# A one-core streaming-encoder step: gating's small products in larger groups, the rows' norm one piece later, k and v copied raw out of PSUM

## The chip, the core and the metric

The kernel runs on one NeuronCore of a Trainium2 chip. The metric is the device time of one execution in microseconds (us). TensorE (PE) multiplies out of SBUF into PSUM; VectorE (DVE), ScalarE (ACT) and GpSimd (POOL) do the elementwise work; SyncE (SP) issues nearly all loads and stores. PEld is TensorE's loading of a stationary operand, which the profile lists apart from the matmul itself. A PSUM tile of 128 x 512 f32 is called a bank here.

## The reference

One layer of a streaming encoder over 256 prompt frames and 64 sample frames (T = 320 columns in all, stored as columns; the 2048 features lie on partitions in 16 tiles of 128):

```python
z = rmsnorm(x, ln_mix_g) @ w_in                  # 2048 -> 3328: q 1024, k 128, v 128, u 1024, v_gate 1024
q, k = rmsnorm(q, q_g), rmsnorm(k, k_g)          # per head of 64
a = windowed_attention(q, k, v, rel_bias, sinks) # 16 heads, 2 kv heads, chunks of 64, band of 192 keys
u, vg = gelu(z_u), rmsnorm(gelu(z_v), g)
s = u * (W_s @ vg + b_s)                         # 8 channel groups, over 128 positions, masked
x = x + concat(rmsnorm(a, g_a), rmsnorm(s, g_s)) @ w_out
x = x + square(relu(rmsnorm(x, ln_ffn) @ w_up)) @ w_down   # 2048 -> 8192 -> 2048
```

Outputs are the new x, the new k and v rows, and the normalised gate rows of the sample frames.

## The kernel before

Every large product keeps 256 output features in PSUM as two banks of 128 x 320 (`acc`, two such tiles in rotation) and reads its weights in **pieces** of 512 features x 256 columns: one DMA (`w_raw`), a rounded copy on ACT (`w_hi`, L108) and the remainder on DVE (`w_lo`, L109), three buffers of each. The activations are split in the same way (XH and XL, FH and FL). A piece is then 24 matmuls of 128x128 by 128x320: 4 feature tiles x 2 halves x 3 terms (hi.hi, hi.lo, lo.hi), all at L134. A product over 2048 features is four pieces.

The program runs in this order. (1) The first pass (L220 to L241) computes q's first 256 columns into `q0_ps` and k and v into `kv_ps`, an `acc` tile, while x itself arrives. (2) `q1`, `q2`, `q3`, each a product of four pieces. (3) Four gate products `v0` to `v3`, then four `u0` to `u3`, each followed by a gelu (`gelu2`). (4) w_out in two halves. (5) The feed-forward, 128 products, with the last one in two separate banks (`apart`).

The small work is fitted **between pieces**: `between_pieces` names, per piece, a function whose matmuls go in behind that piece's 24. `attend(i)` there issues three stages of three different attention blocks: `values_of` (block i-3, L448), `scores` (block i, L392) and `turn` (block i-2, L435, transposes). The last two of them are `attend(11)` and `attend(12)`. Gating's own small work is: `rstd_rows(acc_v)` (L159, the row norm of the gate values, six tiny matmuls and a DVE and a POOL instruction, which give `rv`), `by_rows` (L512, 24 transposes in groups of four, each group into one bank and out by an ACT copy that scales with `rv`), and `spatial` (L526 and L528, three matmuls for each of eight channel groups into one bank, which two DVE additions, L529 and L532, empty). In `u_pieces` the row norm stands directly behind `attend(11)`, at the end of u0.

PSUM is shared out as: two `acc` tiles (four banks), one two-bank tile in the pool `ps_sc` (tag `s_ps`: `q0_ps`, then the scores, and the output `o_ps` of the last attention blocks), and two single banks from `misc()`, for which all other small products take turns.

The mean square of x comes only after the first pass: `rstd` (L167) gives `rx` by a chain of eleven DVE instructions while q1 runs. k and v are multiplied by `rx` out of `kv_ps` (L335, L336), and only then is that `acc` tile free for q2.

Each engine works through its own list in order, and the lists are set when the kernel is built, by a scheduler that estimates times and obeys the hints `issue_after` (behind that instruction in the order; it puts no wait into the program by itself) and `keep_in_program_order`. SP's list is one chain: weight loads with up to four small loads (`between`) behind each.

Of the kernel before, what the change touches and what calls it, by code (L numbers as in the profile page):

```python
# [8 lines left out]
F32 = mybir.dt.float32  # L9
F32R = mybir.dt.float32r  # L10
I32 = mybir.dt.int32
AF = mybir.ActivationFunctionType
ALU = mybir.AluOpType
AX = mybir.AxisListType

P = 128
T = 320
TP = 384
TT = [(0, 128), (128, 128), (256, 64)]
# [4 lines left out]
EPS = 1e-6  # L24
# [6 lines left out]
def hymba_step_kernel(ctx: ExitStack, tc: tile.TileContext, i, o):  # L31
    nc = tc.nc
# [4 lines left out]
    sm = ctx.enter_context(tc.tile_pool(name="sm", bufs=2))  # L37
# [7 lines left out]
    def misc():  # L45
        return ps_m.tile([P, 512], F32, name="misc", tag="misc")
# [9 lines left out]
    xT = const.tile([P, KT, T], F32, name="xT")  # L56
# [5 lines left out]
    tab = const.tile([32, 16], F32, name="tab")  # L62
    oneh = sm.tile([32, 255], F32, name="oneh", tag="w1", bufs=3)
    nc.scalar.dma_start(out=cols, in_=i["cols"])
    nc.gpsimd.dma_start(out=oneh, in_=i["onehot"])
    nc.gpsimd.dma_start(out=tab, in_=i["table"])

    ident = const.tile([P, P], F32, name="ident")
    make_identity(nc, ident)
    nhalf = const.tile([P, 16], F32, name="nhalf")  # L70
    nc.vector.memset(nhalf, -0.5)
    warm = const.tile([P, 1], F32, name="warm")
    nc.scalar.activation(out=warm, in_=nhalf[:, 0:1], func=AF.Exp)
    idle = sm.tile([P, T], F32, name="idle", tag="w1", bufs=3)
    nc.vector.memset(idle, 0.0)
    warm_ps = misc()
    for _ in range(3):
        nc.tensor.matmul(out=warm_ps[:, 0:256], lhsT=idle[:, 0:128], rhs=idle[:, 0:256], start=True, stop=True)
# [119 lines left out]
    def rstd_b(name):  # L198
        return sm.tile([P, T], F32, name=name, tag="rstd_b", bufs=2)
# [16 lines left out]
    kv_ps = acc_tile()  # L216
# [3 lines left out]
    for a, n in [(a, 1) for a in range(8)] + [(a, 2) for a in range(8, KT, 2)]:  # L220
        if a % 4 == 0:
            ahead = blk("w_first", [P, 2, 4, 256])
        raw = ahead[:, :, a % 4:a % 4 + n]
        load(xT[:, a:a + n], xv[:, a:a + n])
        for k in range(n if a else 0):
            load(raw[:, :, k], wv[:, a + k, 0:2048].rearrange("p (j c) -> p j c", j=2)[:, :, 0:256])
        for k in range(a, a + n):
            split(xT[:, k], g_mix[:, k:k + 1], XH[:, k], XL[:, k], pinned=True)
        hi, lo = [t.rearrange("p (j k) c -> p j k c", j=2)[:, :, 0:n] for t in w_tiles()]
        if a:  # L230
            high, low = halves(raw, hi, lo, pinned=True)
        else:
            for j in range(2):
                load(raw[:, j, 0], wv[:, 0, j * 1024:j * 1024 + 256])
                high, low = halves(raw[:, j, 0], hi[:, j, 0], lo[:, j, 0], pinned=True)

        for x, (w_, r_) in enumerate(((hi, xh), (hi, xl), (lo, xh))):
            for j, k, g in [(j, k, g) for j in range(2) for k in range(n) for g in range(2)]:
                ps = q0_ps if j == 0 else kv_ps
                mm = nc.tensor.matmul(out=ps[:, g, 0:T], lhsT=w_[:, j, k, g * P:(g + 1) * P], rhs=r_(a + k),  # L240
                                      start=(a + k == 0 and x == 0), stop=(a + k == KT - 1 and x == 2))  # L241
        steps.append((high, low, mm.ins))
        if a == 5:
            b_ps = misc()
            with tc.issue_after(mm.ins):
                nc.tensor.matmul(out=b_ps[0:16, 0:255], lhsT=tab, rhs=oneh, start=True, stop=True)
        if a == 7:
            b_row = sm.tile([16, 255], F32, name="b_row", tag="w1", bufs=3)
            with tc.issue_after(low):
                nc.vector.tensor_copy(out=b_row, in_=b_ps[0:16, 0:255])  # L250
            b_dram = dram.tile([16, 15, 255], F32, name="b_dram")
            nc.gpsimd.dma_start(out=b_dram, in_=b_row[:, None, :].to_broadcast([16, 15, 255]))
# [9 lines left out]
    vz = kzv[:, 896:1664].rearrange("p (x h d) -> p x h d", x=6, h=2)  # L262
    cv = i["cv"].rearrange("k (h d) -> k h d", h=2)
    vC = vz[:, 5]
    nc.gpsimd.dma_start(out=vC[0:96], in_=cv[0:96])
    sinks = at.tile([P, 8], F32, name="sinks", bufs=1)
    nc.sync.dma_start(out=sinks, in_=i["sinks"])

# [25 lines left out]
    ssq = sums("ssq")  # L294
    nc.vector.tensor_tensor(out=ssq, in0=ssq2[:, 0], in1=ssq2[:, 1], op=ALU.add)

    rk, rx = rstd_b("rk"), rstd_b("rx")

    rq = at.tile([P, 4, 10], F32, name="rq", bufs=1)
# [31 lines left out]
    q1_ps = product(w_in, 0, KT, 256, xh, xl, between_pieces={0: lambda: rstd(ssq, mean_dm, EPS, rx)},  # L331
                    halves_behind={2: lambda: rests[-1]})

    zk = sm.tile([P, T], F32, name="zk", tag="w2", bufs=4)
    nc.vector.tensor_tensor(out=zk, in0=kv_ps[:, 0, 0:T], in1=rx, op=ALU.mult)  # L335
    nc.vector.tensor_tensor(out=vT, in0=kv_ps[:, 1, 0:T], in1=rx, op=ALU.mult)  # L336
    ksq = sums("ksq")
    nc.scalar.activation(out=ksq, in_=zk, func=AF.Square)  # L338
    q0_sq = evict_q(0, q0_ps)
# [114 lines left out]
    def attend(i):  # L454

        for stage, u in ((values_of, i - 3), (scores, i), (turn, i - 2)):
            if 0 <= u < 10:
                with tc.issue_after(narrow[-1]):
                    stage(u)
# [44 lines left out]
    nc.gpsimd.memset(vnat_s[HD:P], 0.0)  # L504
    rv = []

    def by_rows(*ths):

        for t, h in ths:
            (t0, n), vps = TT[t], misc()  # L510
            for a in range(4):
                mm = nc.tensor.transpose(out=vps[0:n, a * P:(a + 1) * P], in_=gv[:, 4 * h + a, t0:t0 + n],  # L512
                                         identity=ident)
            dst = vnat[:, t] if t < 2 else vnat_s[0:HD]
            nc.scalar.activation(out=dst[:, h * 512:(h + 1) * 512], in_=vps[0:n], func=AF.Copy,
                                 scale=rv[0][0:n, t:t + 1])
        narrow.append(mm.ins)
        if ths[-1] == (2, 1):
            nc.gpsimd.dma_start(out=o["sgu_v"], in_=vnat_s[0:HD])

    def spatial(*gs):
        for g in gs:
            sp_ps = misc()
            cs = slice(g * P, (g + 1) * P)
            for b in range(2):
                nc.tensor.matmul(out=sp_ps[:, b * P:(b + 1) * P], lhsT=vnat[:, b, cs], rhs=wsT[:, g], start=True,  # L526
                                 stop=True)
            mm = nc.tensor.matmul(out=sp_ps[:, 256:T], lhsT=vnat_s[:, cs], rhs=wsT[:, g, 0:HD], start=True, stop=True)  # L528
            nc.vector.tensor_tensor(out=gv[:, g, 0:256].rearrange("p (b i) -> p b i", b=2),  # L529
                                    in0=sp_ps[:, 0:256].rearrange("p (b i) -> p b i", b=2),  # L530
                                    in1=sgb[:, g, None, :].to_broadcast([P, 2, P]), op=ALU.add)
            nc.vector.tensor_tensor(out=gv[:, g, 256:T], in0=sp_ps[:, 256:T], in1=sgb[:, g, 0:HD], op=ALU.add)  # L532
        narrow.append(mm.ins)

    def last_values():
        attend(11)
        with tc.issue_after(narrow[-1]):
            rv.append(rstd_rows(acc_v, inv_1k, 4 * EPS))

    acc_s = sums("acc_s")  # L540
    rs_a, rm_a = [], rstd_b("rm_a")
    u_pieces = {
        0: {1: lambda: attend(10), 3: last_values},
        1: {0: lambda: by_rows((0, 0), (1, 0)), 1: lambda: (attend(12), by_rows((2, 0), (0, 1))),
            2: lambda: by_rows((1, 1), (2, 1)), 3: lambda: spatial(0, 1)},
        2: {0: lambda: spatial(2, 3), 1: lambda: spatial(4, 5), 2: lambda: spatial(6, 7)},
        3: {0: lambda: rs_a.append(rstd_rows(acc_a, inv_1k, EPS)), 2: lambda: spread(rs_a[0], rm_a)}}
    gus = {}

# [58 lines left out]
    for b in range(nb):  # L608
        FH = [blk(f"FH{h}", [P, 8, T], F32R) for h in range(2)]
        FL = [blk(f"FL{h}", [P, 8, T], F32R) for h in range(2)]  # L610
        for g in range(FB // 2):
            ps = product(i["w_up"], 0, KT, (b * FB + 2 * g) * P, hh_, hl_, wf)
            t = sm.tile([P, 2, T], F32, name="tf", tag="w2", bufs=4)
            nc.vector.scalar_tensor_tensor(out=t, in0=ps[:, :, 0:T], scalar=0.0, in1=r2[:, None, :].to_broadcast([P, 2, T]),  # L614
                                           op0=ALU.max, op1=ALU.mult)
            nc.scalar.activation(out=t, in_=t, func=AF.Square)
            fs = slice(2 * (g % 4), 2 * (g % 4) + 2)
            fh, fl = FH[g // 4][:, fs], FL[g // 4][:, fs]
            nc.scalar.activation(out=fh, in_=t, func=AF.Copy)
            nc.vector.tensor_tensor(out=fl, in0=t, in1=fh.bitcast(F32), op=ALU.subtract)  # L620
        fh_, fl_ = (lambda k: FH[k // 8][:, k % 8]), (lambda k: FL[k // 8][:, k % 8])
        for g in range(8):
            last, end = b == nb - 1, b == nb - 1 and g == 7
            ps = product(i["w_down"], b * FB, FB, g * 256, fh_, fl_, wf, apart=end)
            parts = [(2 * g, 1, ps[0][:, None, 0:T]), (2 * g + 1, 1, ps[1][:, None, 0:T])] if end else \
                [(2 * g, 2, ps[:, :, 0:T])]
            for a, n, p in parts:
                nc.vector.tensor_tensor(out=xT[:, a:a + n], in0=xT[:, a:a + n], in1=p, op=ALU.add)  # L628
                if last:
                    nc.sync.dma_start(out=yv[:, a:a + n], in_=xT[:, a:a + n])  # L630


def _onehot():
# [63 lines left out]
```

## Time and profile before

| | |
|---|---|
| median of 3 runs | 1252.55 us (1251.66 to 1254.9) |
| the profiled execution | 1251.18 us, of which its span is 1249.4 |
| PE busy | 1243.7 us |
| DVE, ACT, POOL busy | 650.8, 489.4, 102.1 us |
| TensorE clock granted | 1.0 |
| HBM read, written | 182.91 MB, 3.32 MB |

A busy PE in this table isn't PE at its peak: a matmul's row overlaps that of the next. Of use are the starts of its rows, and the chain of waits, in which each row stands from the end of the one before. In a row of the timeline the first number is the start, the second the length, both in us; brackets hold the idle time before it and what ended it.

### The profile page before, as it was taken

How to read it: one execution, taken by the hardware profiler on the slowest of the kernel's cores; microseconds unless marked ns; L12 is line 12 of the kernel's file. 1: busy time of each engine (PE TensorE's matmuls, PEld its weight loads, DVE VectorE, ACT ScalarE, POOL GpSimd, SP SyncE). 2: the span in 40 equal slices, each digit the busy share in tenths (PEclk: the TensorE clock that was granted, in tenths of full speed). 3: DMA queues.
4: the chain of work that ended last, by engine and by line, in shares of the span. 5: the costliest groups of instructions: out<-in, count | busy, mean ns of one | idle time of the engine just before them, and what ended most of it. 6: DMA issues, size and time to landing. Idle time of an engine off the chain costs nothing.

```text
span 1249.4 us, 20216 instructions
## 1 busy us (share of the span) xinstructions
PE 1243.7 (100%) x8519; PEld 1231.9 (99%) x8519; DVE 650.8 (52%) x767; ACT 489.4 (39%) x638; POOL 102.1 (8%) x97
## 2 busy tenths in 40 slices
PE   9999999999999999999999999999999999999998
PEld 8999989999999999999999999999999999999998
DVE  7868675776874444444444444444444444444443
ACT  7345555424544332333344223333332233443221
POOL 1224552301300000000000000000000000000000
PEclk9999999999999999999999999999999999999999
DMA  8644333644554444445544444555444445544550
GB/s 276 208 144 119 102 105 108 220 151 152 152 151 148 151 147 148 152 152 152 151 150 146 148 148 152 152 151 151 150 146 148 149 152 152 152 151 158 169 165 33
DMA packets 186555, 187.78 MB, mean 150 GB/s; under 512 B 6592, under 2 KB 185984, under 8 KB 186464
## 3 DMA queue, kind: packets, MB, share of 16 engines
q1 hardware_dynamic: 185824, 185.43, 47.8%
q8 instruction: 66, 1.08, 0.4%
q0 software_dynamic: 496, 1.03, 0.3%
q14 instruction: 25, 0.20, 0.0%
q10 hardware_dynamic: 144, 0.03, 0.0%
HBM read 182.91 MB, written 3.32 MB: 149 GB/s over the span
## 4 chain that ended last, share of the span: by engine, by line
PE 97%; DMA 2%; SPq 1%; ACT 0%; DVE 0%; issue 0%; ACTq 0%; DVEq 0%
PE acc L134 91%; PE misc L134 1%; DMA w_raw<-in_w_in 1%; SPq L103 1%; PE misc L435 1%; PE s_ps L392 1%; DMA b_dram<-b_row 1%; PE q_ps L240 0%; PE acc L240 0%; PE misc L448 0%; PE misc L314 0%; PE misc L526 0%; PE misc L512 0%; DMA cols<-in_cols 0%; ACT w_hi L108 0%
## 5 line engine op out<-in xcount | busy, mean ns | idle before, releaser
L109 DVE TENSOR_TENSOR w_lo<-w_raw,w_hi 128x1024 fp32r<-128x1024 f32 x332 | 413.7, 1246 | 434.6 <-ACT w_hi L108 425.1
L108 ACT ACTIVATE w_hi<-w_raw 128x1024 fp32r<-128x1024 f32 x332 | 351.8, 1060 | 699.8 <-PE acc L134 660.2
L134 PE MATMUL acc<-H2H,w_hi 128*128 128x320 f32 x1024 | 316.4, 309 | 0.0
L134 PE MATMUL acc<-H2L,w_hi 128*128 128x320 f32 x1024 | 316.4, 309 | 0.0
L134 PE MATMUL acc<-H2H,w_lo 128*128 128x320 f32 x1024 | 316.4, 309 | 0.0
L134 PE MATMUL acc<-FH,w_hi 128*128 128x320 f32 x992 | 306.5, 309 | 0.0
L134 PE MATMUL acc<-FL,w_hi 128*128 128x320 f32 x992 | 306.5, 309 | 0.0
L134 PE MATMUL acc<-FH,w_lo 128*128 128x320 f32 x992 | 306.5, 309 | 0.0
L134 PEld LDWEIGHTS acc<-H2L,w_hi 128*128 128x128 f32 x1024 | 192.3, 188 | 0.0
L134 PEld LDWEIGHTS acc<-H2H,w_hi 128*128 128x128 f32 x1024 | 192.3, 188 | 0.0
L134 PEld LDWEIGHTS acc<-H2H,w_lo 128*128 128x128 f32 x1024 | 192.3, 188 | 0.0
L134 PEld LDWEIGHTS acc<-FH,w_hi 128*128 128x128 f32 x992 | 186.2, 188 | 0.0
L134 PEld LDWEIGHTS acc<-FL,w_hi 128*128 128x128 f32 x992 | 186.2, 188 | 0.0
L134 PEld LDWEIGHTS acc<-FH,w_lo 128*128 128x128 f32 x992 | 186.2, 188 | 0.0
L134 PE MATMUL acc<-XH,w_hi 128*128 128x320 f32 x352 | 111.1, 316 | 0.1
L134 PE MATMUL acc<-XL,w_hi 128*128 128x320 f32 x352 | 108.7, 309 | 0.0
L134 PE MATMUL acc<-XH,w_lo 128*128 128x320 f32 x352 | 108.6, 309 | 0.0
L134 PEld LDWEIGHTS acc<-XH,w_hi 128*128 128x128 f32 x352 | 66.2, 188 | 0.6 <-ACT ksq L338 0.4
L134 PEld LDWEIGHTS acc<-XL,w_hi 128*128 128x128 f32 x352 | 66.2, 188 | 0.0
L134 PEld LDWEIGHTS acc<-XH,w_lo 128*128 128x128 f32 x352 | 66.0, 188 | 0.0
L614 DVE SCALAR_TENSOR_TENSOR tf<-acc,r 128x640 f32<-128x640 f32 x32 | 26.4, 825 | 41.9 <-PE acc L134 41.8
L628 DVE TENSOR_TENSOR xT<-xT,acc 128x640 f32<-128x640 f32 x31 | 25.5, 821 | 41.8 <-PE acc L134 41.8
(206 smaller groups left out, 1054.8 us busy)
## 6 DMA issues: line engine op xcount, KB each, us to landing
w_raw<-in_w_up SPq DMA_DIRECT2D x128, 512.0 KB
w_raw<-in_w_down SPq DMA_DIRECT2D x128, 512.0 KB
w_raw<-in_w_in SPq DMA_DIRECT2D x44, 512.0 KB
w_raw<-in_w_out SPq DMA_DIRECT2D x32, 512.0 KB
w_first<-in_w_in SPq DMA_DIRECT2D x15, 256.0 KB
out_yT<-xT SPq DMA_DIRECT2D x7, 320.0 KB
xT<-in_xT SPq DMA_DIRECT2D x8, 160.0 KB
xT<-in_xT SPq DMA_DIRECT2D x4, 320.0 KB
```

The costliest lines, as they stand in the source:

```text
L103: loads.append(nc.sync.dma_start(out=o_, in_=i_))
L108: return (pin(nc.scalar.activation(out=hi, in_=raw, func=AF.Copy)).ins, pin(nc.vector.tensor_tensor(out=lo, in0=raw, in1=hi.bitcast(F32), ...
L109: pin(nc.vector.tensor_tensor(out=lo, in0=raw, in1=hi.bitcast(F32), op=ALU.subtract)).ins)
L134: mm = nc.tensor.matmul(out=out, lhsT=w_[:, k, g * P:(g + 1) * P], rhs=r_(kk), start=(kk == 0 and x == 0), stop=(kk == nk - 1 and x == 2))
L392: mm = nc.tensor.matmul(out=s_ps[:, p, j * nk:(j + 1) * nk], lhsT=qT[hs, blk_, a:a + 2].rearrange("p a t -> p (a t)"), rhs=kz[hs, kv, k0:k ...
L435: mm = nc.tensor.transpose(out=pt_ps[0:n, (2 * p + j) * P:(2 * p + j + 1) * P], in_=s[:, p, j, c:c + n], identity=ident)
L614: nc.vector.scalar_tensor_tensor(out=t, in0=ps[:, :, 0:T], scalar=0.0, in1=r2[:, None, :].to_broadcast([P, 2, T]), op0=ALU.max, op1=ALU.mult)
L628: nc.vector.tensor_tensor(out=xT[:, a:a + n], in0=xT[:, a:a + n], in1=p, op=ALU.add)
```

## The change

Five things are changed.

1. `rstd_rows(acc_v)` leaves the end of u0 (behind `attend(11)`) and goes one piece later, behind u1's first piece. The transposes of `by_rows`, before in three groups of eight, become a group of sixteen with `attend(12)` behind u1's second piece and one of eight behind its third.
2. `spatial` runs four channel groups at a time, behind u1's last piece and u2's first, in place of two at a time over four pieces. For more than two groups the third and fourth bank are those of the `s_ps` tile (`banks`).
3. k and v are copied out of `kv_ps` by ACT without the norm, into a new tile `kv` (L300 to L302 of the changed kernel); the two multiplications by `rx` then read that tile, and k's is in place.
4. The hints on three small loads on POOL's queue (`onehot`, `table`, the cached values) are later ones; the zeros for the first idle matmuls are written first, and are 256 columns wide.
5. The last output tile is added and stored in two halves of 160 columns, so that there are two DVE additions and two stores where there was one of each.

```diff
-    nc.gpsimd.dma_start(out=oneh, in_=i["onehot"])
-    nc.gpsimd.dma_start(out=tab, in_=i["table"])
-
+
+    idle = sm.tile([P, 256], F32, name="idle", tag="w1", bufs=3)
+    nc.vector.memset(idle, 0.0)
...
+        if a == 1:
+            with tc.issue_after(low):
+                nc.gpsimd.dma_start(out=oneh, in_=i["onehot"])
+                nc.gpsimd.dma_start(out=tab, in_=i["table"])
...
-    nc.gpsimd.dma_start(out=vC[0:96], in_=cv[0:96])
+    with tc.issue_after(steps[-1][1]):
+        nc.gpsimd.dma_start(out=vC[0:96], in_=cv[0:96])
...
+    kv = sm.tile([P, 2, T], F32, name="kv", tag="w2", bufs=4)
+    with tc.issue_after(steps[-1][0]):
+        nc.scalar.activation(out=kv, in_=kv_ps[:, :, 0:T], func=AF.Copy)
...
-    zk = sm.tile([P, T], F32, name="zk", tag="w2", bufs=4)
-    nc.vector.tensor_tensor(out=zk, in0=kv_ps[:, 0, 0:T], in1=rx, op=ALU.mult)
-    nc.vector.tensor_tensor(out=vT, in0=kv_ps[:, 1, 0:T], in1=rx, op=ALU.mult)
+    zk = kv[:, 0]
+    nc.vector.tensor_tensor(out=zk, in0=zk, in1=rx, op=ALU.mult)
+    nc.vector.tensor_tensor(out=vT, in0=kv[:, 1], in1=rx, op=ALU.mult)
...
+    def banks(n):
+
+        if n > 2:
+            ps = ps_sc.tile([P, 2, 512], F32, name="s_ps", tag="s_ps")
+        return [misc() if x < 2 else ps[:, x - 2] for x in range(n)]
+
     def by_rows(*ths):
 
-        for t, h in ths:
-            (t0, n), vps = TT[t], misc()
+        for (t, h), vps in zip(ths, banks(len(ths))):
+            t0, n = TT[t]
...
     def spatial(*gs):
-        for g in gs:
-            sp_ps = misc()
+        for g, sp_ps in zip(gs, banks(len(gs))):
...
-    def last_values():
-        attend(11)
-        with tc.issue_after(narrow[-1]):
-            rv.append(rstd_rows(acc_v, inv_1k, 4 * EPS))
+    def rows_norm():
+        rv.append(rstd_rows(acc_v, inv_1k, 4 * EPS))
...
-        0: {1: lambda: attend(10), 3: last_values},
-        1: {0: lambda: by_rows((0, 0), (1, 0)), 1: lambda: (attend(12), by_rows((2, 0), (0, 1))),
-            2: lambda: by_rows((1, 1), (2, 1)), 3: lambda: spatial(0, 1)},
-        2: {0: lambda: spatial(2, 3), 1: lambda: spatial(4, 5), 2: lambda: spatial(6, 7)},
+        0: {1: lambda: attend(10), 3: lambda: attend(11)},
+        1: {0: rows_norm, 1: lambda: (attend(12), by_rows((0, 0), (1, 0), (2, 0), (0, 1))),
+            2: lambda: by_rows((1, 1), (2, 1)), 3: lambda: spatial(0, 1, 2, 3)},
+        2: {0: lambda: spatial(4, 5, 6, 7)},
...
-            parts = [(2 * g, 1, ps[0][:, None, 0:T]), (2 * g + 1, 1, ps[1][:, None, 0:T])] if end else \
-                [(2 * g, 2, ps[:, :, 0:T])]
-            for a, n, p in parts:
-                nc.vector.tensor_tensor(out=xT[:, a:a + n], in0=xT[:, a:a + n], in1=p, op=ALU.add)
+            parts = [(slice(2 * g, 2 * g + 2), slice(0, T), ps[:, :, 0:T])] if not end else \
+                [(2 * g, slice(0, T), ps[0][:, 0:T])] + \
+                [(2 * g + 1, c, ps[1][:, c]) for c in (slice(0, T // 2), slice(T // 2, T))]
+            for a, c, p in parts:
+                nc.vector.tensor_tensor(out=xT[:, a, c], in0=xT[:, a, c], in1=p, op=ALU.add)
                 if last:
-                    nc.sync.dma_start(out=yv[:, a:a + n], in_=xT[:, a:a + n])
+                    nc.sync.dma_start(out=yv[:, a, c], in_=xT[:, a, c])
```

**ACT at the end of the first pass, before:** two weight copies for q1 stand ahead of the row norm's `n_hl`, and the square of k (`ksq`, L338) stands behind three more.

```order
L108 ACTIVATE w_hi<-w_raw 128x1024 x2
L172 ACTIVATE n_hl<-ssq 128x320
L108 ACTIVATE w_hi<-w_raw 128x1024 x3
L338 ACTIVATE ksq<-zk 128x320
L108 ACTIVATE w_hi<-w_raw 128x1024
L308 ACTIVATE qsq<-qT 128x640
L172 ACTIVATE n_hl<-ksq 128x320
```

The same place in the changed kernel (`kv<-acc` is the new copy of k and v):

```order
L106 ACTIVATE w_hi<-w_raw 128x1024
L302 ACTIVATE kv<-acc 128x640
L170 ACTIVATE n_hl<-ssq 128x320
L106 ACTIVATE w_hi<-w_raw 128x1024 x4
L344 ACTIVATE ksq<-kv 128x320
L314 ACTIVATE qsq<-qT 128x640
L170 ACTIVATE n_hl<-ksq 128x320
```

The new copy and `n_hl` have moved ahead of the weight copy for q1's third piece; the count of weight copies ahead of `ksq` is the same.

**PE at the end of u0, before:** behind u0's last matmul the stages of `attend(11)` (`o_ps` is the output of block 8, `misc<-ident,s` the transposes of block 9) and the row norm, then u1.

```order
L134 MATMUL acc<-XH,w_lo 128x320
L448 MATMUL o_ps<-kzv 64x256 x2
L448 MATMUL o_ps<-vnat,kzv 64x256 x2
L435 MATMUL misc<-ident,s 96x128 x8
L159 MATMUL misc<-inv_1k,acc_v 128x1 x3
L134 MATMUL acc<-XH,w_hi 128x320
```

In the changed kernel the same place:

```order
L132 MATMUL acc<-XH,w_lo 128x320
L454 MATMUL o_ps<-kzv 64x256 x2
L454 MATMUL o_ps<-vnat,kzv 64x256 x2
L441 MATMUL misc<-ident,s 96x128 x8
L132 MATMUL acc<-XH,w_hi 128x320
```

and the two groups behind u1's second piece and its fourth, which hold `attend(12)` with sixteen transposes, and four channel groups of `spatial`:

```order
L454 MATMUL o_ps<-kzv 64x256 x2
L454 MATMUL o_ps<-vnat,kzv 64x256 x2
L524 MATMUL misc<-ident,gv 128x128 x8
L524 MATMUL s_ps<-ident,gv 64x128 x4
L524 MATMUL s_ps<-ident,gv 128x128 x4
...
L537 MATMUL s_ps<-wsT,vnat 128x128 x2
L537 MATMUL misc<-wsT,vnat 128x128 x2
L539 MATMUL misc<-wsT,vnat_s 128x64
L537 MATMUL misc<-wsT,vnat 128x128 x2
L539 MATMUL misc<-wsT,vnat_s 128x64
L539 MATMUL s_ps<-wsT,vnat_s 128x64
```

The row norm no longer stands between the transposes of `attend(11)` and u1, and the third and fourth group of transposes follow `o_ps` into the tile that `o_ps` has just used. Before, the eight channel groups of `spatial` stood on PE as three pairs and, for the last two, one by one, eight matmuls of u2 apart.

**DVE behind u1, in the changed kernel:** from u1's eviction (`z`) on, up to the last addition for the first four channel groups (numbers tell the tiles apart: misc_2246 and misc_2247 are the two single banks, s_ps_2245 the two-bank tile).

```order
L486 TENSOR_TENSOR z_2290<-acc_2074,rx_473 128x640
L107 TENSOR_TENSOR w_lo_2384<-w_raw_2382,w_hi_2383 128x1024
L540 TENSOR_TENSOR gv_1015<-misc_2246,sgb_442 128x256
L543 TENSOR_TENSOR gv_1015<-misc_2246,sgb_442 128x64
L540 TENSOR_TENSOR gv_1015<-misc_2247,sgb_442 128x256
L543 TENSOR_TENSOR gv_1015<-misc_2247,sgb_442 128x64
L489 TENSOR_SCALAR gc_2292<-gc_2292 128x640
L540 TENSOR_TENSOR gv_1015<-s_ps_2245,sgb_442 128x256
L543 TENSOR_TENSOR gv_1015<-s_ps_2245,sgb_442 128x64
L561 SCALAR_TENSOR_TENSOR gv_1015<-gv_1015,gu_2065 128x640
L540 TENSOR_TENSOR gv_1015<-s_ps_2245,sgb_442 128x256
L543 TENSOR_TENSOR gv_1015<-s_ps_2245,sgb_442 128x64
```

Before, the two additions of the first channel group stood ahead of that `w_lo`; now it is ahead of all eight.

More of the change, by code (lines that the diff above doesn't have):

```diff
@@ L73, in hymba_step_kernel @@
     nc.scalar.activation(out=warm, in_=nhalf[:, 0:1], func=AF.Exp)
-    idle = sm.tile([P, T], F32, name="idle", tag="w1", bufs=3)
-    nc.vector.memset(idle, 0.0)
     warm_ps = misc()
```

## The prediction

> **What bounds the kernel now.** I read the page first, then the chain of waits, then TensorE's list of waits, and after that the timeline at the places which the change touches.
>
> ```profile
> span 1249.4 us, 20216 instructions
> PE 97%; DMA 2%; SPq 1%; ACT 0%; DVE 0%; issue 0%; ACTq 0%; DVEq 0%
> ```
>
> In the chain of waits (start, length, what):
>
> ```profile
> 354.37 877.65 PE acc L134 x5984
> ```
>
> The chain is TensorE for 97% of the span, and the feed-forward part of it, 5984 matmuls in 877.65 us, runs at 0.1467 us a matmul without a gap. None of the five edits changes how many such matmuls there are. So what can move is only what lies between them: waits, the small products, the head and the tail. TensorE's waits, by releaser (total, times, longest):
>
> ```profile
> PE misc L78 <- DVE hone L91: 1.3, 1, 1.3
> PE misc L159 <- DVE kzv L437: 0.8, 1, 0.8
> ```
>
> The first is the start of the program. The second is the row norm behind `attend(11)`, which has to have a bank that DVE is still copying out of. A third wait stands under the weight load, before q2:
>
> ```profile
> 49.02 0.31 PE L134 MATMUL acc<-XH,w_lo 128*128 128x320 f32 x1
> 49.47 0.39 PE L134 MATMUL acc<-XH,w_hi 128*128 128x320 f32 x1
> 49.69 0.31 PE L134 MATMUL acc<-XL,w_hi 128*128 128x320 f32 x1
> ...
> 49.44 0.19 PEld L134 LDWEIGHTS acc<-XH,w_hi 128*128 128x128 f32 x1 [0.37 <-ACT ksq L338]
> ...
> 48.44 0.48 DVE L335 TENSOR_TENSOR zk<-acc,rx 128x320 f32<-128x320 f32 x1
> 48.84 0.48 DVE L336 TENSOR_TENSOR kvx<-acc,rx 128x320 f32<-128x320 f32 x1
> ```
>
> Starts that should be 0.147 apart are 0.45 and 0.22 apart there: 0.30 + 0.07 = 0.37 us lost. The profile names `ksq`, but ksq reads only `zk`; what q2 needs is `kv_ps`, and its last reader is L336, which ends at 49.32.
>
> **k and v raw.** ACT's copy takes the place of that release. It can start when the first pass ends:
>
> ```profile
> 34.99 1.06 ACT L108 ACTIVATE w_hi<-w_raw 128x1024 fp32r<-128x1024 f32 x1 [1.71 <-PE acc L240]
> 35.95 0.45 ACT L172 ACTIVATE n_hl<-ssq 128x320 fp32r<-128x320 f32 x1
> ```
>
> ACT stood idle for 1.71 us until the first pass ended at 34.99, so the copy goes in there; 640 columns cost at most the 1.06 us of the 1024 columns of that row, and `kv_ps` is free by about 36, 13 us before q2. Behind it `n_hl` comes at 36.05 at the latest, 0.1 later than now; the weight copy that stood ahead of it, for q1's third piece, ends some 1.1 us later than now, by 37.2. That piece starts two pieces of 24 x 0.147 = 3.52 us and the two matmuls of `rstd` after 35, at about 42. The two multiplications and `ksq` keep their instructions and their places behind the `rx` chain, and now only the norms behind q2's first piece wait for them, 3.5 us after its start. Gain 0.37 us; bounds 0 (some other wait fills the place) and 0.4.
>
> **The row norm one piece later.** The chain of waits from `attend(10)` on; in it each row begins where the one before ended:
>
> ```profile
> 166.24 1.01 PE o_ps L448 x8
> 167.26 1.01 PE misc L435 x8
> 168.27 6.90 PE acc L134 x47
> ...
> 178.99 3.62 PE acc L134 x24
> 182.61 0.87 PE misc L512 x8
> 183.48 3.52 PE acc L134 x24
> 187.01 1.01 PE o_ps L448 x8
> 188.02 1.00 PE misc L512 x8
> ...
> 219.85 0.56 PE misc L159 x6
> ```
>
> `attend(10)` without a norm costs 168.27 - 166.24 = 2.03 us. `attend(11)` with it: one matmul is missing from the row of 47 (two pieces are 48), so it begins at 168.27 + 48 x 0.1467 = 175.31 and ends at 178.99, 3.68 us, and the 24 matmuls behind it take 3.62 in place of 3.52: 3.78 in all. By itself, as the norm of the attention stands at 219.85, it costs 0.56 + 0.1. So 3.78 becomes 2.03 + 0.66 = 2.69: gain 1.09. If it costs its wait-free share here no less than 0.9, the gain is 0.85; I take 1.09, the row of the same instruction. Its bank is then free: TensorE waited 0.8 us for the copy, and now a whole piece, 3.52 us, lies between. What is late next: `r_rows` on DVE, which now stands waiting for that piece; behind it are u0's gelu and a weight remainder for u1's fourth piece, and the gelu's result isn't read before the gate behind u1. The row norm's result has 3.5 us until the transposes' copies need it.
>
> **Larger groups.** Eight transposes cost 0.87 us alone and 1.00 behind `o_ps`. Sixteen with `attend(12)` then cost about 1.00 + 0.8 for the further eight, whose starts are 0.1 us apart, in place of 0.87 + 1.00: gain 0.07. `spatial` before, a pair of channel groups:
>
> ```profile
> 201.78 0.44 PE misc L526 x4
> 202.22 0.17 PE misc L528 x2
> 202.39 0.50 PE misc L526 x4
> 202.89 0.17 PE misc L528 x2
> 203.06 3.57 PE acc L134 x24
> ```
>
> A group that opens costs 0.44 + 0.17 and 0.05 of the next 24; one that follows costs 0.50 + 0.17. So 0.66 against 0.67: merging two into four saves nothing by these rows. I take 0, and -0.1 to +0.2 as its bounds.
>
> The two places where a new wait can arise are the banks of `s_ps`. First, the third group of transposes needs `o_ps` emptied by ACT:
>
> ```profile
> 186.95 1.06 ACT L108 ACTIVATE w_hi<-w_raw 128x1024 fp32r<-128x1024 f32 x1 [1.73 <-issue]
> 188.07 0.38 ACT L451 ACTIVATE ao<-o_ps 128x256 f32<-128x256 f32 x1
> ```
>
> ACT is done with it at 188.45, 1.44 us after the small products began at 187.01; TensorE gets there after 1.01 + about 0.85. So 0.4 us are to spare. Second, u2's group of four needs the banks that DVE empties behind u1:
>
> ```profile
> L480 DVE TENSOR_TENSOR z<-acc,rx 128x640 f32<-128x640 f32 x8 | 6.6, 823 | 7.8 <-PE acc L134 7.8
> L529 DVE TENSOR_TENSOR gv<-misc,sgb 128x256 f32<-128x256 f32 x8 | 3.4, 420 | 3.4 <-PE misc L528 3.2
> L532 DVE TENSOR_TENSOR gv<-misc,sgb 128x64 f32<-128x64 f32 x8 | 1.7, 215 | 0.0
> L552 DVE SCALAR_TENSOR_TENSOR gv<-gv,gu 128x640 f32<-128x640 f32 x4 | 3.3, 820 | 0.1
> L109 DVE TENSOR_TENSOR w_lo<-w_raw,w_hi 128x1024 fp32r<-128x1024 f32 x332 | 413.7, 1246 | 434.6 <-ACT w_hi L108 425.1
> ```
>
> z 0.82, one w_lo 1.25, four additions of 0.64, the gelu's middle step (under 0.82) and the gate 0.82 are at most 6.3 us. TensorE spends 2.7 us on the first four groups, 3.6 on a piece and 1.3 on the two single banks before it needs `s_ps` again: 7.6. So this too is hidden, with 1.3 us to spare.
>
> **Head and tail.**
>
> ```profile
> GB/s 276 208 144 119 102 105 108 220 151 152 152 151 148 151 147 148 152 152 152 151 150 146 148 148 152 152 151 151 150 146 148 149 152 152 152 151 158 169 165 33
> ...
> 0.75 2.63 DMA cols<-in_cols
> ...
> 4.32 1.43 PE q_ps L240 x4
> ...
> 1.30 0.74 POOL L65 DMA_DIRECT2D oneh<-in_onehot  x1 [0.85 <-POOLq L681]
> ...
> 1246.14 0.49 DVE xT L628
> ```
>
> The start waits for `cols`, and the small loads only move behind a few fills on POOL, with no wait on the weights; their 34 KB are 0.12 us at the 276 GB/s of the first slice (the page's row of rates). I take 0 for the head, with 0.1 of gain as its bound. At the end one addition of 0.49 us becomes two of 0.22 (64 columns) to 0.42 (256 columns) each; the first store goes earlier, the last one 0 to 0.3 us later with half the bytes. I take 0, bounds -0.3 and +0.2.
>
> **Sum.** 0.37 + 1.09 + 0.07 = 1.53 us off the profiled execution, whose own time is 1251.18: 1249.65, a span of 1247.9. The median of the runs shown is 1252.55, 1.37 above it; I add that and predict **1251.0 us**. That is 0.12% less. A change of under 0.3% (3.8 us) isn't told from none in this kernel, whose three runs are 3.2 us apart.
>
> **Rivals.**
>
> *A wait at `s_ps` (slower).* If ACT empties `o_ps` late behind u1's second piece, TensorE stands in the middle of its sixteen transposes. For it: the weight copy stands directly ahead of that eviction, and now one bank more hangs on it. Against it: 0.4 us to spare, and that copy has waited for TensorE and not for its load. Its price is ACT's lateness less 0.4; from 1.9 us of lateness on, the changed kernel is slower than before. With the copy held for as long as the one at 34.99 was, 1.71, the sum is 0.2 us of gain, 1252.3; with twice that, 3.4, it is 1254.0. I give it 0.08.
>
> *The wait only moves.* TensorE gets to u1 1.7 us sooner, while DVE's copies of the last transposes, u0's eviction and the remainders come no sooner; if u1's first pieces then wait for these, the 1.09 is gone and what remains is 0.44: 1252.1. For it: DVE was the one that TensorE waited for there. Against it: u1 reads no result of those copies, and its weights are prepared up to three pieces ahead. 0.10.
>
> *The clock rises sooner.* The first four matmuls take 1.43 us, 0.36 each, against 0.147 later, so something at the start is slow; the idle matmuls now begin sooner. If the four ran at full pace, 0.84 us would go, to 1250.2. The profile's granted clock reads 1.0 there, so no row tells when this ends. 0.05. [...]
>
> *Transposes slow what follows.* The longest stretch of small products grows from 2.0 to about 2.8 us. If TensorE's clock fell behind it, 24 matmuls would take 0.36 each and not 0.147, 5 us more: 1256. Against it: behind the 2.0 us stretch at 187.01, the next pieces run at 3.52 us. 0.03. [...]
>
> My forecast has the remaining 0.74.
>
> **How the numbers follow.** The terms' bounds give gains of 0.4 to 2.1 us, 1250.4 to 1252.2 on the scale of the median. Medians of a few runs wander by about 1 us here (1251.66 to 1254.9 in three), and the rivals reach to 1254. The range is 1249.2 to 1253.6. Faster by over 0.3% needs 1248.8 or less, which no case gives without the wandering: 0.08. Slower by over 0.3% needs 1256.3: the last rival and the far end of the first, 0.04. The rest, 0.88, is no change that can be told.
>
> **What would show it.** In the changed profile TensorE's list of waits should have no row for the row norm; the matmuls around q2's start should be 0.147 us apart; `attend(11)` should cost 2.0 us, the sixteen transposes with `attend(12)` some 2.8, and each `spatial` group of four 2.6 to 2.7. A wait of the `s_ps` transposes for ACT would show the first rival. A span under 1246 or over 1249.4 would make the sum wrong.

## The result, and the profile after

The changed kernel takes 1260.38 us (median of six runs, 1260.19 to 1260.48), beside 1252.11 us for the kernel before (median of six, 1251.44 to 1254.9). The ratio is 1.0062, interval 1.005 to 1.0075: it is slower, by 8.3 us. I had predicted 1251.0. Its profiled execution took 1260.34 us with a span of 1258.6, against a span of 1249.4 before.

TensorE's list of waits in the changed kernel (total, times, longest, in us):

```profile
PE s_ps L537 <- DVE gv L543: 6.0, 2, 4.0
PE s_ps L524 <- ACT vnat_s L527: 1.7, 1, 1.7
PE misc L76 <- DVE hone L89: 1.2, 1, 1.2
PE acc L238 <- ACT w_hi L106: 0.2, 1, 0.2
```

The row norm's wait (0.8 us, L159 before) is gone, as forecast. In its place stand three waits at `s_ps`, 7.7 us together, and all three have one form. TensorE's timeline around them (start, length, what, the idle time before it):

```profile
186.14 0.60 PE L524 MATMUL s_ps<-ident,gv 128*64 128x128 f32 x4
188.40 0.66 PE L524 MATMUL s_ps<-ident,gv 128*128 128x128 f32 x4 [1.66 <-ACT vnat_s L527]
...
201.02 0.71 PE L537 MATMUL s_ps<-wsT,vnat 128*128 128x128 f32 x4 [2.10 <-DVE gv L543]
...
206.59 0.66 PE L537 MATMUL s_ps<-wsT,vnat 128*128 128x128 f32 x4
207.09 0.33 PE L539 MATMUL s_ps<-wsT,vnat_s 128*128 128x64 f32 x2
211.38 1.22 PE L537 MATMUL s_ps<-wsT,vnat 128*128 128x128 f32 x4 [3.95 <-DVE gv L543]
```

Each time the products into one bank of the tile have run, and those into the other bank stand and wait, not for the tile's former owner but for a copy that empties the bank just filled. Here is that copy at the first of the three places, in ACT's timeline, and at the third, in DVE's:

```profile
186.74 0.46 ACT L480 ACTIVATE sq<-ao 128x320 f32<-128x320 f32 x1
187.10 0.68 ACT L527 ACTIVATE vnat<-misc,rs_rows 128x512 f32<-128x512 f32 x1
187.67 0.67 ACT L527 ACTIVATE vnat_s<-s_ps,rs_rows 64x512 f32<-64x512 f32 x1
189.10 0.69 ACT L527 ACTIVATE vnat<-s_ps,rs_rows 128x512 f32<-128x512 f32 x1 [0.75 <-PE s_ps L524]
```

```profile
205.96 0.82 DVE L492 SCALAR_TENSOR_TENSOR gu<-gc,z 128x640 f32<-128x640 f32 x1 [2.68 <-ACT gc L491]
206.82 1.37 DVE L561 SCALAR_TENSOR_TENSOR gv<-gv,gu 128x640 f32<-128x640 f32 x1
...
208.58 1.21 DVE L107 TENSOR_TENSOR w_lo<-w_raw,w_hi 128x1024 fp32r<-128x1024 f32 x1
...
210.78 0.41 DVE L540 TENSOR_TENSOR gv<-s_ps,sgb 128x256 f32<-128x256 f32 x1
211.12 0.21 DVE L543 TENSOR_TENSOR gv<-s_ps,sgb 128x64 f32<-128x64 f32 x1
212.96 0.42 DVE L540 TENSOR_TENSOR gv<-s_ps,sgb 128x256 f32<-128x256 f32 x1 [1.63 <-PE s_ps L539]
```

ACT works through its list in order, so the copy of the third group of transposes comes behind two squares and the two copies of the single banks; it ends at 188.34, and at 188.40 TensorE goes on. At the third place DVE had itself stood for 2.68 us until `gc` came from ACT; then the gate (L561), a weight remainder, the additions for the single banks and a step of the attention's split (L203) came first, and the additions that TensorE waits for end at 211.33. In the program text of `by_rows` and `spatial`, the copy of a group stands between its products and those of the next group. With one bank to a tile that was harmless; the two halves of `s_ps` are one tile.

The third wait has a sequel. Some of the windows that one view of the changed kernel cuts (us; then PE's busy time, and behind the engines the granted clock, the DMA share and GB/s):

```profile
183.00:205.00 22.00, 18.24 (x135) 17.11 (x134) 9.91 (x16) 11.29 (x20) 7.00 (x8) 1.00 0.38 108
...
212.00:214.00 2.00, 2.00 (x10) 2.00 (x10) 0.56 (x2) 0.00 (x0) 0.00 (x0) 0.50 0.52 182
...
217.00:220.00 3.00, 3.00 (x23) 3.00 (x22) 0.64 (x1) 1.06 (x1) 0.00 (x0) 1.00 0.00 0
```

and its matmuls at the end of that stretch, first 0.27 us apart and then 0.15:

```profile
216.29 0.47 PE L132 MATMUL acc<-XL,w_hi 128*128 128x320 f32 x1
216.56 0.47 PE L132 MATMUL acc<-XH,w_lo 128*128 128x320 f32 x1
...
217.04 0.31 PE L132 MATMUL acc<-XL,w_hi 128*128 128x320 f32 x1
217.19 0.31 PE L132 MATMUL acc<-XH,w_lo 128*128 128x320 f32 x1
```

From the end of the wait, 211.38, to 217.04, TensorE ran at half its clock (0.50 in the window 212 to 214, 1.00 in that from 217 on). In these 5.66 us it got through sixteen matmuls of 320 columns and the six small ones of a channel group. At full pace they take about 3.1 us: 16 x 0.147, and 0.67 + 0.05 for the group by the prediction's rows. So some 2.6 us are lost. Behind the waits of 1.66 and 2.10 us the clock stayed at 1.00 (the window 183 to 205).

Since the start of the program differs from one execution to the next (in the ten traces the norm of x starts at 37.7 to 40.0 us), I compare the kernels from the norm of x on, where the first pass is over: the span's end less the start of the first matmul of `rstd` (L175 before, L173 after).

```profile
38.32 0.31 PE L175 MATMUL misc<-n_hl,mean_dm 128*128 128x320 f32 x1
```

```profile
37.92 0.31 PE L173 MATMUL misc<-n_hl,mean_dm 128*128 128x320 f32 x1
```

Before, 1249.4 - 38.3 = 1211.1 us; after, 1258.6 - 37.9 = 1220.7. So 9.6 us were added behind that point, which itself came 0.4 us earlier. The spans differ by 9.2 us and the medians by 8.3, since the profiled execution before, 1251.18 us, lies 0.9 under its median. I call this stretch **the rest**. It is from one trace for each kernel; executions that ought to agree do so to 0.3 us (e1, e2, f3 and f4 below: 1209.6 to 1209.9).

### The profile page after: what moved, and what is told of

The parts are those of the page before. It is cut to its first block, busy times and chain, and to the rows that moved or that the text cites. A ratio compares the mean times of both kernels' runs of the same rounds, so it can differ in the third digit from the quotient of the medians.

```text
span 1258.6 us, 20213 instructions
## 1 busy us (share of the span) xinstructions
PE 1245.9 (99%) x8519; PEld 1234.0 (98%) x8519; DVE 651.9 (52%) x768; ACT 490.2 (39%) x639; POOL 102.1 (8%) x97
## 3 DMA queue, kind: packets, MB, share of 16 engines
q0 software_dynamic: 496, 1.03, 0.3%
## 4 chain that ended last, share of the span: by engine, by line
PE 98%; DVE 1%; ACT 1%; DMA 0%; issue 0%; SPq 0%; DVEq 0%; ACTq 0%
PE acc L132 92%; PE acc L238 1%; PE misc L132 1%; PE q_ps L238 1%; PE misc L441 1%; PE s_ps L398 1%; PE misc L454 0%; PE misc L320 0%; DMA w_first<-in_w_in 0%; PE o_ps L454 0%; DVE w_lo L107 0%; DVE gv L540 0%; ACT sq L480 0%; DVE gv L561 0%; ACT w_hi L106 0%
```

## The experiments

None of these kernels leaves out any work. Those of a batch share one chip and the runs of the kernel before: median 1251.89 us of 33 in the first batch (e1 to e4), 1252.18 of 33 in the second (f1 to f4).

### e1: all products of a group first, then the copies

```diff
-        for (t, h), vps in zip(ths, banks(len(ths))):
+        groups = list(zip(ths, banks(len(ths))))
+        for (t, h), vps in groups:
             t0, n = TT[t]
             for a in range(4):
                 mm = nc.tensor.transpose(...)
+        for (t, h), vps in groups:
+            t0, n = TT[t]
             dst = vnat[:, t] if t < 2 else vnat_s[0:HD]
             nc.scalar.activation(...)
...
-        for g, sp_ps in zip(gs, banks(len(gs))):
+        groups = list(zip(gs, banks(len(gs))))
+        for g, sp_ps in groups:
...
+        for g, sp_ps in groups:
             nc.vector.tensor_tensor(...)
```

> The changed kernel with one edit: by_rows and spatial issue all matmuls of a group first and the copies out of the banks after them; banks, groups and places are the same. Theory A (order in the program): the two halves of the s_ps tile are one thing to the program's bookkeeping, so a matmul into the second half, issued behind the first half's copy, has to wait for that copy. Then the three waits (1.66 + 2.10 + 3.95 us) and the half clock behind the longest vanish and the kernel takes 1250 to 1251 us, 0.1 to 0.2% under the kernel before. Theory B (the banks come free too late, DVE is behind): the s_ps banks of u2's group of four are still emptied late, TensorE waits 2 to 4 us there, and the time is 1254 to 1258.

Measured: 1249.53 us (median of 11, 1249.17 to 1251.8), ratio 0.9982 (0.9973 to 0.999): faster than both kernels, 2.4 us under the one before and a little under theory A's range. TensorE's whole list of waits:

```profile
PE misc L76 <- DVE hone L89: 1.2, 1, 1.2
PE q_ps L238 <- ACT w_hi L106: 0.2, 1, 0.2
```

In the chain of waits the two places now read, without a gap:

```profile
176.00 1.01 PE o_ps L454 x8
...
181.54 0.56 PE misc L157 x6
...
185.73 1.01 PE o_ps L454 x8
186.74 1.02 PE misc L525 x8
187.77 0.87 PE s_ps L525 x8
188.64 3.52 PE acc L132 x24
...
196.56 0.45 PE s_ps L541 x4
...
199.01 0.17 PE s_ps L543 x2
...
219.51 0.56 PE misc L157 x6
```

The granted clock is 1.000 over the span. The groups, their sizes and their banks are those of the changed kernel; only the order of products and copies is another. So the loss is neither the size of the groups nor the late emptying of the tile by its former owner.

### e2: the order as changed, but two tiles of one bank each

```diff
-    q0_ps = ps_sc.tile([P, 2, 512], F32, name="q0_ps", tag="s_ps")
+    def sc(p, name):
+        return ps_sc.tile([P, 512], F32, name=name, tag=f"s{p}")
+
+    q0_ps = [sc(0, "q0_ps"), sc(1, "q0_ps")]
...
-        if n > 2:
-            ps = ps_sc.tile([P, 2, 512], F32, name="s_ps", tag="s_ps")
-        return [misc() if x < 2 else ps[:, x - 2] for x in range(n)]
+        return [misc() if x < 2 else sc(x - 2, "s_ps") for x in range(n)]
```

(The scores and `o_ps` take the two tiles likewise, and q0's eviction becomes two instructions.)

> The changed kernel with its order of matmuls and copies as it is, but the two banks of s_ps are two tiles of one bank each (q0's eviction is two instructions for it). Theory A (bookkeeping by tile): no wait between the two banks, 1250 to 1251.5 us. Theory B (banks late): 1254 to 1258, as the banks and their readers are the same.

Measured: 1251.11 us (median of 10, 1249.07 to 1251.39), ratio 0.9988 (0.9979 to 0.9997), inside theory A's range. The row of e1's list for L76 is the only one in TensorE's list here: no wait at the two tiles. The rest takes 1209.8 us, as in e1 (1209.7). The scheduler did not keep the order everywhere, though: the second group of transposes in `s_ps` went behind twelve matmuls of u1's third piece (the two groups start at 187.95 and 190.15). So e2 doesn't test the first place with the changed kernel's order. At `spatial` the products stand in the changed kernel's order, and those for the second of the two tiles start 1.7 us before the first addition out of the first one:

```profile
198.69 0.66 PE L543 MATMUL s_ps<-wsT,vnat 128*128 128x128 f32 x4
```

```profile
200.35 0.41 DVE L546 TENSOR_TENSOR gv<-s_ps,sgb 128x256 f32<-128x256 f32 x1
```

So for these two places the banks and the copies' order in the program alone make no wait; it takes both that the halves are one tile and that the first half's copy stands ahead of the second half's products. For the first place e1 shows the order, and that the tile counts there too is argued from the same form.

### e3 and e4: one wait after the other

e3 keeps the sixteen transposes and takes `spatial` back to pairs:

```diff
-            2: lambda: by_rows((1, 1), (2, 1)), 3: lambda: spatial(0, 1, 2, 3)},
-        2: {0: lambda: spatial(4, 5, 6, 7)},
+            2: lambda: by_rows((1, 1), (2, 1)), 3: lambda: spatial(0, 1)},
+        2: {0: lambda: spatial(2, 3), 1: lambda: spatial(4, 5), 2: lambda: spatial(6, 7)},
```

> The changed kernel with spatial in pairs of channel groups over four pieces as before; by_rows keeps its sixteen transposes with two of its groups in s_ps. Theory A: the wait of 1.7 us in the transposes stays, those of 2.1 and 4.0 and the slow clock go: 1252 us, no difference to before that can be told. Theory B: the time is governed by DVE behind u1, which now has its work spread as before, so it is also about 1252, but then the wait in the transposes should be gone or under 0.5 us.

Measured: 1251.61 us (median of 10, 1251.03 to 1253.59), ratio 0.9998 (0.9989 to 1.0007). Only the wait of 1.7 us is left at `s_ps`, as theory A says.

e4 keeps the first group of four channel groups too and takes only the second back to pairs:

```diff
-        2: {0: lambda: spatial(4, 5, 6, 7)},
+        2: {0: lambda: spatial(4, 5), 1: lambda: spatial(6, 7)},
```

> The changed kernel with only the first four channel groups of spatial as a group of four; the other four come in pairs. Theory A: waits of 1.7 and 2.1 us stay, the 4.0 goes. If the clock falls only behind a wait of about 4 us, the granted clock stays 1.0 and the time is 1254 us; if a wait of 2 us is enough (rival), the clock falls behind this one and the time is 1256.

Measured: 1254.88 us (median of 10, 1253.26 to 1255.62), ratio 1.0019 (1.001 to 1.0028). Its waits at `s_ps`, and TensorE's clock over the whole place (the last three numbers are the clock, DMA share and GB/s):

```profile
PE s_ps L537 <- DVE gv L543: 2.1, 1, 2.1
PE s_ps L524 <- ACT vnat_s L527: 1.7, 1, 1.7
```

```profile
183.00:222.00 39.00, 35.24 (x258) 34.11 (x257) 21.07 (x34) 19.68 (x32) 12.74 (x13) 1.00 0.30 88
```

The waits are those of theory A, and the time lies between its 1254 and the rival's 1256. The ten executions show a part of why: four, the profiled one among them, took 1253.3 to 1253.7 us at a mean clock of 1.000, and six took 1254.8 to 1255.6. Of these six, two read a mean clock of 0.999 and two 0.998. If the lower clock is the 0.50 of the changed kernel's trace, a mean of 0.998 is by its rounding at least 3.8 us at half clock (0.0015 x 1253 / 0.5). A mean of 1.000, which the traced executions of all kernels but the changed one read, is at most 1.25 us (0.0005 x 1250 / 0.5), and in the changed kernel's trace 0.6 us at half clock lies behind the last matmul. So in some executions of e4 the clock did fall, and the rival isn't refuted; no trace shows where. Two of the six read 1.000, and their time stays open. The ladder below goes by the profiled execution, in which the clock stayed up.

With e1 the four kernels make a ladder, in which each step adds one wait:

| kernel | waits at `s_ps` | the rest, us | added |
|---|---|---|---|
| e1 | none | 1209.7 | |
| e3 | 1.66 | 1211.6 | 1.9 |
| e4 | 1.66 + 2.10 | 1213.9 | 2.3 |
| changed kernel | 1.66 + 2.10 + 3.95, and the clock | 1220.7 | 6.8 |

A wait of the first two costs its idle time and 0.2 us more. The rows suggest why: a row of four small products is 0.60 us long, and where nothing waits the next begins 0.44 behind its start, so a wait also costs that overlap. The last step, 6.8, is by the same count 3.95 + 0.2 + 2.6: the wait, the overlap and the half clock behind it. The kernel before stands at 1211.1, so e1's 1.4 us of gain and the steps' 11.0 us of loss make the 9.6.

### f1 to f4: what the small edits are worth by themselves

f1 is the kernel before with the edits of the start alone (the later hints of the three small loads, the narrower zeros):

```diff
-    nc.gpsimd.dma_start(out=oneh, in_=i["onehot"])
-    nc.gpsimd.dma_start(out=tab, in_=i["table"])
+    idle = sm.tile([P, 256], F32, name="idle", tag="w1", bufs=3)
+    nc.vector.memset(idle, 0.0)
...
+        if a == 1:
+            with tc.issue_after(low):
+                nc.gpsimd.dma_start(out=oneh, in_=i["onehot"])
+                nc.gpsimd.dma_start(out=tab, in_=i["table"])
...
+    with tc.issue_after(steps[-1][1]):
+        nc.gpsimd.dma_start(out=vC[0:96], in_=cv[0:96])
```

> The kernel before with the change's edits of the start alone (later hints for the small loads, zeros for the idle matmuls first and 256 wide). Forecast's reading: nothing to be told, within 0.1% of before. Rival (the clock rises sooner with earlier idle matmuls): in the profiles seen so far the first pass reached the bias matmul at 15.6 to 15.8 us in three runs with this start, at 17.3 and 17.6 in two, and at 16.2 in the one without it; if the start decides which, the median is 0.4 to 0.6 us under before, and without it (e1 with the old start) the quicker executions are missing.

Measured: 1250.84 us (median of 11, 1250.4 to 1252.31), ratio 0.9987 (0.9978 to 0.9996): 1.34 us under its kernel before, more than either reading forecast. The idle matmuls begin hardly earlier, at 1.20 us in place of 1.29. The rest takes 1210.7, 0.4 less than before, and TensorE's gap before q2 is gone although k and v still leave PSUM through `rx`. DVE's timeline shows how:

```profile
46.97 0.48 DVE L339 TENSOR_TENSOR kvx<-acc,rx 128x320 f32<-128x320 f32 x1
...
48.10 1.21 DVE L107 TENSOR_TENSOR w_lo<-w_raw,w_hi 128x1024 fp32r<-128x1024 f32 x1
```

The scheduler has put k's and v's multiplications (the first row shown is v's) ahead of a weight remainder, and `kv_ps` is free at 47.45, where the kernel before freed it at 49.32.

f2 is the kernel before with the raw copy of k and v alone:

```diff
+    kv = sm.tile([P, 2, T], F32, name="kv", tag="w2", bufs=4)
+    with tc.issue_after(steps[-1][0]):
+        nc.scalar.activation(out=kv, in_=kv_ps[:, :, 0:T], func=AF.Copy)
...
+    zk = kv[:, 0]
+    nc.vector.tensor_tensor(out=zk, in0=zk, in1=rx, op=ALU.mult)
+    nc.vector.tensor_tensor(out=vT, in0=kv[:, 1], in1=rx, op=ALU.mult)
```

> The kernel before with the raw copy of k and v alone. The term of the sum: the wait of 0.37 us ahead of q2 goes, the matmuls there are 0.147 us apart, and nothing else moves: 0.4 us or 0.03% less, which the times can hardly tell and the trace can. Rival: the wait for it moves to the norms behind q2's first piece, and nothing is gained.

Measured: 1251.09 us (median of 11, 1250.65 to 1252.74), ratio 0.999 (0.9981 to 0.9999); the rest 1210.7, 0.4 less than before, so the wait didn't move to the norms. In ACT's timeline the copy takes 0.68 us and not up to 1.06, and it stands behind one weight copy (in the changed kernel it comes at the end of the first pass, at 34.65, where I had put it):

```profile
36.00 0.68 ACT L299 ACTIVATE kv<-acc 128x640 f32<-128x640 f32 x1
```

The two edits take away the same 0.4 us; together they give it once (the rest of f4 below, without the new start, is within 0.3 us of e1's). By the medians f1 and f2 gain 1.34 and 1.09 us. What the 0.7 to 0.9 us beyond the rest's 0.4 come from is not shown: the profiled execution before lies about 1 us under its median, so its one trace may not stand for the others.

f3 is e1 with the last output tile in one piece, as before:

```diff
-            parts = [(slice(2 * g, 2 * g + 2), slice(0, T), ps[:, :, 0:T])] if not end else \
-                [(2 * g, slice(0, T), ps[0][:, 0:T])] + \
-                [(2 * g + 1, c, ps[1][:, c]) for c in (slice(0, T // 2), slice(T // 2, T))]
+            parts = [(2 * g, 1, ps[0][:, None, 0:T]), (2 * g + 1, 1, ps[1][:, None, 0:T])] if end else \
+                [(2 * g, 2, ps[:, :, 0:T])]
```

> The changed kernel with all products of a group first, and the last tile in one piece as before. From the last matmul's start to the end of the span the kernel before takes 3.61 us, the four kernels with two halves 3.66 to 3.72: the tail in one piece is worth 0.05 to 0.1 us, 1249.4 us. Rival (the second half's smaller store pays): 0.1 us or more slower than in halves.

Measured: 1249.62 us (median of 11, 1249.08 to 1252.26), ratio 0.9979 (0.997 to 0.9988), beside e1's 1249.53 in the other batch. The rest takes 1209.6. From the last matmul's start to the end of the span it is 3.59 us, in e1 3.66. The halves are worth nothing that can be told.

f4 is e1 with the start of the kernel before, that is f1's edit undone:

```diff
+    nc.gpsimd.dma_start(out=oneh, in_=i["onehot"])
+    nc.gpsimd.dma_start(out=tab, in_=i["table"])
...
-        if a == 1:
-            with tc.issue_after(low):
-                nc.gpsimd.dma_start(out=oneh, in_=i["onehot"])
-                nc.gpsimd.dma_start(out=tab, in_=i["table"])
```

> The changed kernel with all products of a group first, and the start as before. If the start is worth nothing, 1249.5 to 1250 us as with the new one; if the earlier idle matmuls decide when the clock rises, 0.4 to 2 us more.

Measured: 1250.35 us (median of 11, 1249.58 to 1252.44), ratio 0.9988 (0.9979 to 0.9997); the rest 1209.9. This is the raw copy, the later norm, the larger groups and the tail in halves, without the waits and without the new start: 1.83 us under its kernel before. By the medians the new start adds up to 0.8 us, but the start differs between executions by more than that (last section), so this figure is weak.

## Why the prediction was wrong

**What bounds the kernel** was read rightly: TensorE's chain, in which only waits and small products can move. It is why 7.7 us of new waits came out whole in the time.

**k and v raw: 0.37 us.** From the norm of x to q2's first piece it measured 0.38 (f2), inside the bounds. What the step did not see is that this gap hung on DVE's order of instructions and not on the copy alone: the start edits move it away too (f1). I had costed those at nothing.

**The row norm one piece later: 1.09 us, and larger groups: 0.07.** In e1's chain `attend(11)` begins at 176.00 and the attention's norm ends at 220.07, 44.07 us. Before, by the prediction's rows, it begins at 175.31 and ends at 220.41, 45.10. So 1.03 of the forecast 1.16 came, inside the bounds. The norm by itself costs 0.56 + 0.1 and `attend(11)` 2.02, as said. Sixteen transposes with `attend(12)` cost 2.91 (185.73 to 188.64), where I had 2.8; four channel groups 2.63 (196.56 to 199.19), where I had 2.6 to 2.7.

**The step that failed** is the paragraph on "the two places where a new wait can arise". For both I asked when the tile's former owner is gone ("0.4 us are to spare", "hidden, with 1.3 us to spare"), and for neither whether the second half of a group waits for the first half of the same group. It does: the products of the fourth bank wait for the copy of the third, since the copy stands between them in the program and the tile is one for the bookkeeping. The order of the copies, which I had looked at on DVE, even gave the lateness, for the copy of the third bank stands behind those of the two single banks, a weight remainder and a step of the gelu. What I had held to be slack for TensorE was its wait. e1 shows that the order makes the waits, e2 that the tile has its part in those at `spatial`, and the ladder shows the price: 1.9 + 2.3 + 6.8.

**The rivals.** "A wait at `s_ps`" had the place right and the mechanism wrong: ACT's eviction of `o_ps` was not late (it started at 185.32, 1.1 us behind the start of the small products). Its price was bounded by lateness of that one copy, so the rival ended at 1254. Its sign, a wait of these transposes for ACT, came, but for another copy. "Transposes slow what follows" had the kind of loss right, a clock that falls, but its size (5 us, where some 2.6 were lost) and its trigger wrong: in e1's trace the sixteen transposes do nothing to the clock (the 24 matmuls behind them take 3.52 us), and in the changed kernel it falls within the wait of 3.95 us. I had no case that held a wait and the clock together, which is the one that came. "The wait only moves" did not come.

**Head and tail: 0.** The tail is 0.1 us longer by the trace and tells nothing in the times. The head's edits have an effect I had not costed, through the scheduler's order.

With the failed step mended, the sum holds by the traces: the forecast was 1.53 us less for the terms that it counted, against 1.4 us in e1's rest. By the medians f4 gains 1.83 us and e1 2.4; that surplus, like the one of f1 and f2, stays open.

## What to carry to other kernels

Before giving several groups of products the parts of one tile, write down the order of products and copies within the group: if the first part is copied out ahead of the second part's products, these wait for that copy (1.66, 2.10 and 3.95 us here). Issue all products first, or make each part a tile of its own. Price a new wait by where the copy stands in its engine's queue, and add the clock if TensorE's idle time goes beyond the 2.10 us behind which it stayed at 1.00 in these traces: in the wait of 3.95 us it fell after 2.7.

## What the runs showed of the hardware

**The clock after a wait.** In the traces TensorE's clock stayed at 1.00 behind idle times of 1.66 and 2.10 us and read 0.50 for 5.66 us behind one of 3.95 us; no run had a wait between 2.10 and 3.95. It fell within that wait: the last product ends at 207.42, and two narrow windows of the changed kernel, with the clock as the third number from the end, read

```profile
210.05:210.10 0.05, 0.00 (x0) 0.00 (x0) 0.05 (x2) 0.00 (x0) 0.05 (x1) 1.00 0.00 0
210.15:210.20 0.05, 0.00 (x0) 0.00 (x0) 0.05 (x2) 0.00 (x0) 0.05 (x1) 0.50 0.00 0
```

So 2.7 us without a matmul were enough here, and the half clock stood for 6.8 us, to 217.0. Behind the last matmul of the program, which ends at 1255.19, the clock of the changed kernel falls too, after 2.8 us: it reads 1.00 to 1258.00 and 0.50 from 1258.05 on. In the trace before it reads 1.00 to the end of the span, 3.3 us behind the last matmul. What sets the idle time that is enough isn't shown. That 2.10 us are always safe isn't shown either: four of e4's executions read a mean clock under 1.000, and so do four of the 33 before in each batch, whose longest wait in the trace behind the start is 0.8 us.

**The pace at the start.** In nine of the ten traces the first matmuls of the first pass run at about half pace, and where that ends differs between executions; in f2's they run at full pace from the first, at 4.37 us. In the chains of the changed kernel and of e1, whose starts have the same instructions:

```profile
5.82 0.85 PE acc L238 x4
6.67 0.29 PE q_ps L238 x2
```

```profile
5.85 1.44 PE acc L238 x4
7.29 0.53 PE q_ps L238 x2
...
9.42 0.37 PE q_ps L238 x2
```

Two matmuls take 0.29 us at full pace and 0.53 before. The changed kernel's profiled execution got there before 5.9 us, for the first four of its row take 0.85 us where e1's take 1.44; e1's got there at about 9.4, and the norm of x starts at 37.9 against 39.4. The granted clock doesn't show the change of pace: it reads 1.00 from 4.30 to 5.00 and from 5.80 to 6.50 in the changed kernel, and 1.00 from 4.30 to 10.00 in the trace before, whose matmuls also begin at half pace. e1's profiled execution took 1251.71 us, one of two of its eleven above 1251; the other nine took 1249.2 to 1249.7. That fits a rise of the pace that comes some 3.5 us later and costs half of that, and so do e2 and f3, whose profiled executions also start late (norm of x at 39.7 and 40.0, the others' at 37.7 to 38.3) and whose rests are that of e1. But the other executions leave no trace, so this is argued and not shown, and whether the new start makes the late case more frequent stays open.

**VectorE and GpSimd at the same time.** The gate, which takes 0.82 us before, took 1.93 us in the changed kernel, while POOL ran a step of the gelu. DVE's and POOL's timelines of the changed kernel:

```profile
200.88 1.93 DVE L561 SCALAR_TENSOR_TENSOR gv<-gv,gu 128x640 f32<-128x640 f32 x1
206.82 1.37 DVE L561 SCALAR_TENSOR_TENSOR gv<-gv,gu 128x640 f32<-128x640 f32 x1
```

```profile
200.59 1.53 POOL L490 TENSOR_TENSOR gc<-gc,z 128x640 f32<-128x640 f32 x1 [4.54 <-DVE gc L489]
...
205.08 2.43 POOL L481 TENSOR_TENSOR acc_a<-acc_a,sq 128x320 f32<-128x320 f32 x2
```

Both gates end 0.7 us after the POOL instruction that had begun before them: 202.81 against 202.12, and 208.19 against 207.51. These 0.7 us are nearly the gate's own 0.82, so my reading is that it began its work about when POOL was done; what holds it isn't shown. The other order is in the trace before: its first gate began ahead of POOL, at 200.23, and took 0.82 us, and POOL's step of the gelu, begun at 200.41, took 2.07 us in place of the 1.53 above. I had taken 0.82 us for the gate; by the order of the rows the added 1.1 us made the copy of the first four's last bank later, and ACT's chain to `gc`, for which DVE then stood 2.68 us ahead of the third wait; that share wasn't tried by itself.
